# Hybrid decoder layer on one Trainium2 core: one 384-byte pair of buffers leaves an early pool, and a 0/1 matrix is loaded with the tables and rounded by GpSimd

## The chip, the cores and the metric

The kernel runs on one core of one Trainium2 chip. The metric is the device time of one execution in microseconds (us), as the median of several runs. Five engines work side by side, each on its own queue and in the order that the program gives it: TensorE (PE, matmul; its weight loads are a row of their own, PEld), VectorE (DVE), ScalarE (ACT), GpSimd (POOL) and SyncE (SP), which issues every DMA of this kernel.

## The reference

One layer (DEPTH is 1) over x of shape (1, 2048, 1024), float32. After an RMSNorm one projection gives 13 slices of 256 channels, which four token mixers share:

```
h = _rms_norm(x, pre_g)
proj = jnp.einsum('bsd,de->bse', h, w_in)
aq, ak, av, ag, bu, bv, bg, cx, cg, dq, dk, dv, dg = jnp.split(proj, N_IN_SLICES, axis=-1)
ya = _dilated_mixture(heads(aq), heads(ak), heads(av))
yb = _spatial_gating(bu, bv, sgu_g, sgu_w, sgu_b)
yc = _multiscale_pool(cx, pool_w, pool_scale)
yd = _retention(dq, dk, dv, ret_g)
y = jnp.concatenate([ya * jax.nn.silu(ag), yb * jax.nn.silu(bg),
                     yc * jax.nn.silu(cg), yd * jax.nn.silu(dg)], axis=-1)
return x + _rms_norm(jnp.einsum('bse,ed->bsd', y, w_out), post_g)
```

Mixer A, the one that matters here, is softmax attention with 4 heads of 64 channels, each in three dilations (1, 4, 16). The three results of a head are added with weights that come from their log-sum-exp values: `o = sum over g of softmax(lse)[g] * out[g]`.

## The kernel before

Everything is float32, and a product is made of three matmuls: each operand is split into a rounded high part (type float32r) and the low rest, and high*high, high*low and low*high are added in PSUM. A matrix whose entries are 0 and 1 needs no low part; it is only copied into a float32r tile.

Stage 1 (function bodies up to line 538) makes all projections, in two halves of 1024 tokens. `prologue` normalizes and transposes x into tiles `hh` and `hl` (pool `big`); `weights` (L237) loads a slice of w_in into `raw`, and ACT and DVE split it into `w128` or `w256`; `proj_t` (L257) multiplies with the weights as the stationary operand and 512 tokens of `hh` as the moving one, `proj_m` (L267) with `hh` stationary and 256 columns of weights moving. The last two parts of the second half are `c_mix` (L384: pooling on POOL, tiles `c_x` and `c_s`, then `c_pl` on DVE, L412) and `a_gate` (L328: SiLU of the gate into `ag_s`, stored to DRAM as `agd`, L334).

Stage 2 (L880 to L898) is the attention. `attention(p, tab)` does two heads: it loads `q2`, `k2a`, `k2b` and the values `att_v` of a head (L569 to L585, seven buffers of 8 KB under one tag), and calls `branch` for the dilations 4, 16 and 1. In a branch PE makes scores (`ps_s`), DVE adds the bias and takes the row maximum (L649), ACT takes the exponential (L651), PE transposes (`ps_pt`), ACT and DVE split the result into `pt_hi` and `pt_lo` (L658, L659), and PE multiplies with the values (`ps_o`). `att_p`, the tile of the probabilities, has six buffers under the tag `pr` of pool `p2`. After the third dilation `weigh` (L744) turns the statistics into weights: a row of small DVE operations on 128x16 and 128x48, among them the rounding of `ew` into `eh` (L761, L762), ending in tile `wt`.

`combine` (L768) spreads these weights over the channels: it transposes `wt` to `wr` (32 rows) and multiplies `wr` with `sel`, a 32 x 8 x 128 matrix of zeros and ones, `mm(F, sel[:, n % 8], wr[g], True, True)` (L784), and DVE multiplies the attention results with F. So `sel` is first needed when the first pair of heads is done. It is loaded between `attention(0, tab)` and `combine(0, ...)` (L887 to L890) in two halves: a DMA each into a 2 KB buffer of the tag `pr`, and a DVE copy each into `sel`. A pool gives the buffers of one tag out in the order of the program, so these two take their turn behind all `att_p` tiles of `attention(0, tab)`.

Between the attention's matmuls PE is given output projections that don't need mixer A: `partial(t)` (L841) for 9 of the 16 token tiles, each held back by `tc.issue_after` until a chosen matmul of `attention(1, tab)`. Its weights `wo` come from `out_weights` (L545): two DMAs of 512 KB into `wo_raw` (tag `z` of pool `p3`, two buffers of 4 KB), a rounding by ACT (L551) and a subtraction by POOL or DVE (L552). Stage 3 (from L900) combines the second pair and finishes all tiles in `final`.

The order on each queue is set by a list scheduler that plans with modelled durations: an instruction is written into its engine's queue when the plan has it ready, earlier lines of the program first. On the chip each engine then follows that order, and waits where an input is late. DMAs share eight completion semaphores in turn, so a DMA also waits until the eighth before it has landed.

Pools are stacked from both ends of a partition's memory. From the left stand `const`, `big`, `small`, and above them in stage 1 `pa`, `pd`, `p1`, in stage 2 `pm`, `p2`, in stage 3 `p4`; from the right `k1` in stage 1 and later `p3`, `po`, `pc`. A tile that takes over memory waits for the last use of the tiles that were there. As the program before is laid out (byte addresses in a partition): `small` 82560 to 85952, its last tag `eh` with two buffers of 192 bytes; `w256` at 118720; `raw` at 153536 and 157632; six 2 KB buffers of the tag `w2` (among them `c_y`, `ag_s`) from 169920; `w128` at 182208, 190400, 198592; `c_x` 206784 to 208896; `c_s` 208896 to 213120. On the right: `sel` 174304, `wt`, `wr`, `sga` up to 184288; `po` up to 208864; the two `z` buffers at 208864 and 212960; and of stage 1 `cm`, the table whose last reader is `c_pl`, at 214816.

Of the kernel before, what the change touches and what calls it, by code (L numbers as in the profile page):

```python
# [9 lines left out]
F32 = mybir.dt.float32  # L10
F32R = mybir.dt.float32r
# [7 lines left out]
P = 128  # L19
SEQ = 2048  # L20
DM = 1024
KT = DM // P
GRP = 512
# [10 lines left out]
C_ID, C_DEC, C_ZETA, C_XI, C_CD, C_INVP, C_CNT, C_SEL, C_MIX = 0, 128, 640, 896, 1152, 1408, 1410, 1442, 2466  # L34
# [6 lines left out]
B_PR, B_PT = 6, 3  # L41
# [47 lines left out]
def hymba(ctx: ExitStack, tc: tile.TileContext, x, pre_g, w_in, sgu_g, sgu_w, sgu_b, pool_w,  # L89
          pool_scale, ret_g, w_out, post_g, cmix, catt, out, dbg=None, npart=9, spread=(0.3, 0.95)):  # L90
    nc = tc.nc
    V, A, G, T, D = nc.vector, nc.scalar, nc.gpsimd, nc.tensor, nc.sync

    def r32(ap):
        return ap.bitcast(F32)
# [4 lines left out]
    def transpose(o, i, n=P):  # L100
        T.transpose(o, i, ident[:n, :n])  # L101
# [3 lines left out]
    small = ctx.enter_context(tc.tile_pool(name="small", bufs=2))  # L105
# [435 lines left out]
    p3 = ctx.enter_context(tc.tile_pool(name="p3", bufs=1, side="right", reuse_waits="tile"))  # L541
# [15 lines left out]
    def attention(p, tab):  # L557
        o01 = (big if p == 0 else po).tile([P, 2, SEQ], F32, tag="big" if p == 0 else "o01", name="att_o01")
        o2 = po.tile([P, SEQ], F32, tag="o2", name="att_o2")
        o = [o01[:, 0], o01[:, 1], o2]  # L560
        wt = pc.tile([P, 3, 2, 2, 2, 8], F32, tag="wt", bufs=1, name="wt")
        for s in range(2):
            h = 2 * p + s
            rows = slice(s * HD, (s + 1) * HD)
            other = slice((1 - s) * HD, (2 - s) * HD)
            q2 = pm.tile([P, SEQ], F32R, tag="m8", bufs=7, name="q2")
            k2a = pm.tile([P, SEQ], F32R, tag="m8", bufs=7, name="k2a")
            k2b = pm.tile([P, SEQ], F32R, tag="m8", bufs=7, name="k2b")
            D.dma_start(r32(q2[rows]), qk_d[0][p][rows, 0])  # L569
            D.dma_start(r32(q2[other]), qk_d[0][p][rows, 1])  # L570
            for z in (rows, other):
                D.dma_start(r32(k2a[z]), qk_d[1][p][rows, 0])
                D.dma_start(r32(k2b[z]), qk_d[1][p][rows, 1])
            for b, dil in enumerate(DILS):
                vt = pm.tile([P, 16, 2 * HD], F32R, tag="m8", bufs=7, name="att_v")
                dst = r32(vt)
                if dil == 1:
                    src = v_d[h].rearrange("(n t c) d -> c t n d", c=4, t=32)
                    for c in range(4):
                        D.dma_start(dst[c * 32:(c + 1) * 32], src[c])  # L580
                elif dil == 4:
                    D.dma_start(dst.rearrange("q (j c) d -> q j (c d)", j=4),
                                v_d[h].rearrange("(j q c) d -> q j (c d)", j=4, c=4))
                else:
                    D.dma_start(dst.rearrange("q r d -> q (r d)"), v_d[h].rearrange("(q r) d -> q (r d)", r=16))  # L585
                qb = q2
                if dil != 1:
                    qb = pm.tile([P, SEQ], F32R, tag="m8", bufs=7, name="q2b")
                    if dil == 4:
                        src = r32(q2).rearrange("p (j k c i) -> p c j k i", j=4, c=4, i=8)  # L590
                        dst = qb.rearrange("p (j c k i) -> p c j k i", j=4, c=4, i=8)
                        for c in range(4):
                            (V if c < 3 else G).tensor_copy(dst[:, c], src[:, c])
                    else:
                        V.tensor_copy(qb.rearrange("p (r w i) -> p r w i", r=16, i=8),
                                      r32(q2).rearrange("p (w r i) -> p r w i", r=16, i=8))
                if dil == 1:
                    sv = p2.tile([P, 3, 2, 16], F32, tag="sv", bufs=2, name="sv")
                    raw = p2.tile([64, P], F32, tag="sT", bufs=1, name="sraw")
                    D.dma_start(raw, st_d[h].rearrange("b z (n q) -> (b z n) q", q=P))  # L600
                    branch(h, dil, qb, k2a, k2b, vt, tab, o[b], sv[:, b])
                    weigh(sv, raw, wt[:, :, :, s])
                    continue
                st = p2.tile([P, 2, 16], F32, tag="stat", bufs=2, name="att_st")
                branch(h, dil, qb, k2a, k2b, vt, tab, o[b], st)
                keep_stats(h, b, dil, st)
        return o01, o2, wt
# [121 lines left out]
    def keep_stats(h, b, dil, st):  # L729

        pt = ps2.tile([P, GRP], F32, tag="t", bufs=N_T, name="ps_st")
        transpose(pt[:32, :P], st.rearrange("p z n -> p (z n)"))
        sT = p2.tile([32, P], F32, tag="sT", bufs=1, name="sT")
        V.tensor_copy(sT, pt[:32, :P])
        for z in range(2):
            dst, src = st_d[h][b, z], sT[z * 16:(z + 1) * 16]
            if dil == 4:
                for j in range(4):
                    D.dma_start(dst.rearrange("(j k c i) -> j c k i", j=4, k=16, c=4)[j],
                                src[j * 4:j * 4 + 4].rearrange("c (k i) -> c k i", i=8))  # L740
            else:
                D.dma_start(dst.rearrange("(w r i) -> r w i", r=16, i=8), src.rearrange("r (w i) -> r w i", i=8))

    def weigh(sv, raw, w):  # L744

        pt = ps2.tile([P, GRP], F32, tag="t", bufs=N_T, name="ps_sv")
        transpose(pt[:, :64], raw, 64)
        V.tensor_copy(sv[:, :2].rearrange("q b z n -> q (b z n)"), pt[:, :64])
        nm = small.tile([P, 16], F32, tag="nm", name="nm")
        V.tensor_tensor(nm, sv[:, 0, 0], sv[:, 1, 0], ALU.min)  # L750
        V.tensor_tensor(nm, nm, sv[:, 2, 0], ALU.min)
        df = small.tile([P, 3, 16], F32, tag="df", name="df")
        V.tensor_tensor(df, sv[:, :, 0], nm.unsqueeze(1).broadcast_to([P, 3, 16]), ALU.subtract)
        ew = small.tile([P, 3, 16], F32, tag="ew", name="ew")
        A.activation(ew, df, AF.Exp, scale=-1.0)
        V.tensor_tensor(df, ew, sv[:, :, 1], ALU.mult)
        V.tensor_tensor(nm, df[:, 0], df[:, 1], ALU.add)
        V.tensor_tensor(nm, nm, df[:, 2], ALU.add)
        V.reciprocal(nm, nm)
        V.tensor_tensor(ew, ew, nm.unsqueeze(1).broadcast_to([P, 3, 16]), ALU.mult)  # L760
        eh = small.tile([P, 3, 16], F32R, tag="eh", name="eh")  # L761
        V.tensor_copy(eh, ew)  # L762
        V.tensor_copy(w[:, :, :, 0], r32(eh).rearrange("q b (g n) -> q b g n", g=2))
        for b in range(3):
            V.tensor_tensor(w[:, b, :, 1], ew[:, b].rearrange("q (g n) -> q g n", g=2),
                            r32(eh[:, b]).rearrange("q (g n) -> q g n", g=2), ALU.subtract)
# [111 lines left out]
    pc = ctx.enter_context(tc.tile_pool(name="pc", bufs=1, side="right", reuse_waits="tile"))  # L878
    sel = pc.tile([32, 8, P], F32R, name="sel")
    with ExitStack() as c2:  # L880
        pm = c2.enter_context(tc.tile_pool(name="pm", bufs=1, reuse_waits="tile"))
        p2 = c2.enter_context(tc.tile_pool(name="p2", bufs=1, reuse_waits="tile"))
        ps2 = c2.enter_context(tc.tile_pool(name="ps2", bufs=2, space=PSUM, reuse_waits="tile"))
        tab = pm.tile([P, T_HEAD], F32, name="tab")
        D.dma_start(tab, catt)
        o = attention(0, tab)
        for z in range(2):  # L887
            raw = p2.tile([P, 4, P], F32, tag="pr", bufs=B_PR, name="sel_raw")[:32]
            D.dma_start(raw, cmix[:32, C_SEL + z * GRP:C_SEL + (z + 1) * GRP].rearrange("r (n m) -> r n m", m=P))
            V.tensor_copy(sel[:, z * 4:z * 4 + 4], raw)  # L890
        for i in (1, 2, 3):
            out_weights(i, V if i == 2 else G)
        combine(0, o, ps2, "t", False, range(0, SEQ, GRP), G)
        o = attention(1, tab)
        for t in range(npart):
            with tc.issue_after(marks[int(len(marks) * (t + spread[0]) / npart * spread[1])]):
                partial(t)
        out_weights(0, G)  # L898
# [13 lines left out]
    for i, t in enumerate(full):  # L912
        n = -(-len(have) // (len(full) - i))
# [30 lines left out]
```

## Time and profile before

| what | value |
|---|---|
| median of 3 runs | 1067.3 us |
| lowest and highest | 1065.59 and 1068.7 us |
| the profiled execution | 1072.46 us |
| its span, first to last instruction | 1070.8 us |
| mean granted TensorE clock | 0.977 |
| PE busy | 1013.1 us, 95% of the span |
| DVE, ACT, POOL busy | 521.2, 377.4, 226.5 us |
| DMA | 128.91 MB, mean 120 GB/s |

The page of the profile shows one execution. A busy row counts an instruction from its start to its modelled end, and matmuls overlap, so 95% does not mean that PE is at its peak. The chain is the work that ended last, followed back from the last instruction to what released each step. In timelines a row gives start, duration, engine, line, operation, output and inputs, count, and in brackets how long the engine stood idle before it and what it waited for. The granted clock is the share of TensorE's full clock that it was allowed. Stage 1 ends at about 690 us, stage 2 at about 940 us.

### The profile page before, as it was taken

To read this page: it belongs to the slowest core of one execution; us is meant where nothing else is said; L and a number is where in the kernel's file an instruction comes from. 1 tells how busy PE (TensorE), PEld (TensorE's weight loads), DVE (VectorE), ACT (ScalarE), POOL (GpSimd) and SP (SyncE) were. 2 spreads that over 40 slices of the span, in tenths; PEclk is the share of its full clock that TensorE was granted. 3 is DMA by queue.
4 is the path that set the end of the run, shared out by engine and by line. 5 is a ranking of instruction groups with operands and counts; after the bars stand their busy time and mean duration, and the time that the engine had idled before them with its cause. 6 is when DMAs were issued, how large, how long until landed. Compare 5 with 4: busy or idle time off the path is not lost.

```text
span 1070.8 us, 15827 instructions
## 1 busy us (share of the span) xinstructions
PE 1013.1 (95%) x5960; PEld 862.7 (81%) x5960; DVE 521.2 (49%) x1586; ACT 377.4 (35%) x871; POOL 226.5 (21%) x216
## 2 busy tenths in 40 slices
PE   5899999999999999999999999997989989999995
PEld 5888898888777988989898777786987979866774
DVE  7511215686323331031675312177766767737766
ACT  6320213132212331132211111397763878712231
POOL 2310002121133000002120134031115521213444
PEclk9999999999999999999999999997899989999998
DMA  8530222332323232041311650286475573445566
GB/s 279 145 98 21 79 80 79 119 119 63 115 78 89 89 99 59 1 144 44 109 60 39 155 175 28 72 215 174 100 213 129 140 226 76 140 153 178 172 246 216
DMA packets 111036, 128.91 MB, mean 120 GB/s; under 512 B 9904, under 2 KB 89008, under 8 KB 108912
## 3 DMA queue, kind: packets, MB, share of 16 engines
q1 hardware_dynamic: 110960, 127.90, 40.0%
q8 instruction: 47, 0.77, 0.3%
q14 instruction: 29, 0.24, 0.1%
HBM read 91.57 MB, written 36.31 MB: 119 GB/s over the span
## 4 chain that ended last, share of the span: by engine, by line
PE 82%; DMA 9%; DVE 5%; issue 1%; POOL 1%; ACT 1%; SPq 1%; DVEq 0%; POOLq 0%; ACTq 0%
PE ps_t L98 38%; PE ps_m L98 15%; PE ps_out L98 11%; PE ps_s L98 4%; PE ps_o L98 4%; PE ps_pt L101 3%; PE ps_of L98 2%; DMA k2b<-qk 2%; DMA out_dram<-z 1%; DMA cm<-in_cmix_dram 1%; DMA z<-partd 1%; DMA sel_raw<-in_cmix_dram 1%; DMA raw<-in_w_in_dram 1%; PE ps_in L98 1%; DVE z L872 1%
## 5 line engine op out<-in xcount | busy, mean ns | idle before, releaser
L98 PE MATMUL ps_t<-hh,w 128*128 128x512 f32 x1152 | 372.8, 400 | 0.0
L98 PEld LDWEIGHTS ps_t<-hh,w 128*128 128x128 f32 x1152 | 215.9, 188 | 54.0 <-issue 3.4
L98 PE MATMUL ps_t<-hl,w 128*128 128x512 f32 x576 | 229.0, 398 | 0.0
L98 PE MATMUL ps_m<-w,hh 128*128 128x256 f32 x1024 | 187.8, 283 | 3.8 <-ACT hh L232 3.8
L98 PEld LDWEIGHTS ps_m<-w,hh 128*128 128x128 f32 x1024 | 159.1, 190 | 5.4 <-ACT hh L232 4.4
L98 PE MATMUL ps_out<-wo,yt 128*128 128x512 f32 x576 | 156.6, 411 | 0.7 <-DVE z L872 0.6
L98 PE MATMUL ps_m<-w,hl 128*128 128x256 f32 x512 | 146.4, 286 | 0.1
L98 PEld LDWEIGHTS ps_t<-hl,w 128*128 128x128 f32 x576 | 108.3, 188 | 26.1 <-issue 1.4
L98 PEld LDWEIGHTS ps_out<-wo,yt 128*128 128x128 f32 x576 | 106.6, 194 | 24.8 <-issue 2.8
L252 DVE TENSOR_TENSOR w<-raw,w 128x1024 fp32r<-128x1024 f32 x42 | 58.4, 1399 | 110.6 <-ACT w L250 110.6
L98 PEld LDWEIGHTS ps_m<-w,hl 128*128 128x128 f32 x512 | 97.3, 190 | 0.7 <-DVE hl L233 0.3
L649 DVE CUSTOM_DVE_ANT_0 att_p<-ps_s,tab 128x128 f32<-128x128 f32 (+1 forms) x192 | 60.8, 360 | 39.1 <-PE ps_s L98 32.9
L250 ACT ACTIVATE w<-raw 128x1024 fp32r<-128x1024 f32 (+1 forms) x56 | 55.0, 997 | 70.3 <-PE ps_t L98 38.2
L659 DVE TENSOR_TENSOR pt_lo<-ps_pt,pt_hi 128x512 fp32r<-128x512 f32 x80 | 51.4, 651 | 18.2 <-ACT pt_hi L658 17.6
L651 ACT ACTIVATE att_p<-att_p,att_st 128x128 f32<-128x128 f32 (+1 forms) x128 | 55.0, 432 | 10.3 <-DVE att_st L649 9.9
L98 PE MATMUL ps_o<-pt_hi,att_v 128*128 128x128 f32 (+1 forms) x204 | 52.6, 280 | 3.1 <-DVE att_o L674 3.1
L98 PE MATMUL ps_o<-pt_lo,att_v 128*128 128x128 f32 (+1 forms) x204 | 52.3, 293 | 3.3 <-DVE pt_lo L659 3.3
L101 PE MATMUL ps_pt<-ident,att_p 128*128 128x128 f32 x300 | 50.9, 286 | 1.5 <-ACT att_p L651 1.3
L446 POOL TENSOR_TENSOR d_g<-d_g,ret_b 128x512 f32<-128x512 f32 x8 | 10.4, 1294 | 185.6 <-ACT d_g L444 185.6
L658 ACT ACTIVATE pt_hi<-ps_pt 128x512 fp32r<-128x512 f32 x80 | 44.2, 565 | 12.9 <-PE ps_pt L101 7.7
L98 PEld LDWEIGHTS ps_o<-pt_hi,att_v 128*128 128x128 f32 x204 | 40.2, 197 | 5.5 <-DVE att_o L674 3.6
L98 PEld LDWEIGHTS ps_o<-pt_lo,att_v 128*128 128x128 f32 x204 | 40.2, 197 | 5.0 <-DVE pt_lo L659 3.8
(174 smaller groups left out, 1414.3 us busy)
## 6 DMA issues: line engine op xcount, KB each, us to landing
raw<-in_w_in_dram SPq DMA_DIRECT2D x52, 512.0 KB
qk<-qk_s SPq DMA_DIRECT2D x16, 512.0 KB
att_v<-vd SPq DMA_DIRECT2D x8, 1024.0 KB
xr<-in_x_dram SPq DMA_DIRECT2D x16, 512.0 KB
out_dram<-z SPq DMA_DIRECT2D x15, 512.0 KB
xt<-in_x_dram SPq DMA_DIRECT2D x7, 1024.0 KB
yraw<-yb SPq DMA_DIRECT2D x16, 384.0 KB
partd<-z SPq DMA_DIRECT2D x9, 512.0 KB
```

Of the source, the lines that this page charges most:

```text
L98: return T.matmul(o, lhsT, rhs, start=start, stop=stop, skip_group_check=True)
L101: T.transpose(o, i, ident[:n, :n])
L250: A.activation(hi, raw[:, :, cs], AF.Copy, scale=sc)
L252: eng.tensor_tensor(lo, raw[:, :, cs], r32(hi), ALU.subtract)
L446: G.tensor_tensor(o, o, ret_b.unsqueeze(1).broadcast_to([P, 2, 256]), ALU.mult)
L649: V.tensor_tensor_reduce(out=pr[:, u, :w], in0=ps[:, u, :w], in1=bb, scale=-SLOPES[h] * HD ** -0.5, scalar=3e38, op0=ALU.add, op1=ALU.min, ...
L651: A.activation(pr[:, u, :w], pr[:, u, :w], AF.Exp, bias=neg, scale=-1.0, accum_out=st[:, 1, n:n + 1])
L658: A.activation(hi, pt[:, :w], AF.Copy)
L659: V.tensor_tensor(lo, pt[:, :w], r32(hi), ALU.subtract)
L872: V.scalar_tensor_tensor(z[:, ns], ps, rstd, post_b[:, ns], ALU.mult, ALU.mult)
```

## The change

`eh` leaves pool `small`, where it had two buffers, for pool `pc`, where it has one. Everything that is stacked above `small` on the left moves down by 384 bytes, the weights `w128` and `w256` of the projections among it, while `hh` and `hl` stay; on the right `pc` grows by 192 bytes. The load of `sel` goes from behind `attention(0, tab)` to a place ahead of it, next to the load of `tab`; it becomes one DMA of 32 rows of 4 KB into a buffer of the tag `z` of `p3`, and the two DVE copies become one POOL copy.

```
@@ weigh
-        eh = small.tile([P, 3, 16], F32R, tag="eh", name="eh")
+        eh = pc.tile([P, 3, 16], F32R, tag="eh", bufs=1, name="eh")
         V.tensor_copy(eh, ew)
@@ stage 2
         tab = pm.tile([P, T_HEAD], F32, name="tab")
         D.dma_start(tab, catt)
+        raw = p3.tile([P, DM], F32, tag="z", bufs=2, name="sel_raw")[:32]
+        D.dma_start(raw, cmix[:32, C_SEL:])
+        G.tensor_copy(sel, raw.rearrange("r (n m) -> r n m", m=P))
         o = attention(0, tab)
-        for z in range(2):
-            raw = p2.tile([P, 4, P], F32, tag="pr", bufs=B_PR, name="sel_raw")[:32]
-            D.dma_start(raw, cmix[:32, C_SEL + z * GRP:C_SEL + (z + 1) * GRP].rearrange("r (n m) -> r n m", m=P))
-            V.tensor_copy(sel[:, z * 4:z * 4 + 4], raw)
         for i in (1, 2, 3):
             out_weights(i, V if i == 2 else G)
```

## The prediction

> **What bounds the kernel now.** I read the page first, then the chain of waits in order of time, then the timelines of DVE, PE, SP and POOL where the chain leaves PE.
>
> ```profile
> span 1070.8 us, 15827 instructions
> PE 82%; DMA 9%; DVE 5%; issue 1%; POOL 1%; ACT 1%; SPq 1%; DVEq 0%; POOLq 0%; ACTq 0%
> ```
>
> PE carries 82% of the chain and DMA 9%. So a change pays in two ways only: PE does its work faster, or one of the few places goes where PE waits for something else. The chain in order of time names such a place, and it is the load that the change moves:
>
> ```profile
> 789.70 10.04 DMA sel_raw<-in_cmix_dram
> ...
> 799.76 0.75 DVE sel L890 x2
> ...
> 800.54 0.70 DVE pt_lo L659
> ...
> 801.28 1.22 PE ps_o L98 x4
> ```
>
> The reader sees a row of dependents: the load lands 10.04 us after its issue, only then can DVE round it into `sel`, only then does DVE reach the `pt_lo` that stood behind in its queue, and PE's `ps_o` waits for that. Nothing needs `sel` yet: its first matmul comes at 814.7, by the tile's own answer.
>
> ```profile
> L98 PE MATMUL ps_f<-wr,sel x32: 326/422/442, 814.7 to 992.0; 32*128 32x384 f32 x32
> ...
>   DMA sel_raw<-in_cmix_dram: 5.4, 1
> ```
>
> The same place in the timelines of DVE, ACT and PE gives the price to DVE and to PE (in brackets the idle time ahead and its end):
>
> ```profile
> 799.76 0.75 DVE L890 CAST sel<-sel_raw 32x512 fp32r<-32x512 f32 x2 [5.39 <-DMA sel_raw<-in_cmix_dram]
> 800.54 0.69 DVE L659 TENSOR_TENSOR pt_lo<-ps_pt,pt_hi 128x512 fp32r<-128x512 f32 x1
> ...
> 794.80 0.98 ACT L658 ACTIVATE pt_hi<-ps_pt 128x512 fp32r<-128x512 f32 x2 [1.15 <-PE ps_pt L101]
> ...
> 797.93 0.27 PE L98 MATMUL ps_o<-pt_hi,att_v 128*128 128x256 f32 x1
> 801.28 0.58 PE L98 MATMUL ps_o<-pt_lo,att_v 128*128 128x256 f32 x1 [3.08 <-DVE pt_lo L659]
> ```
>
> And the stretches around it, as columns PE, PEld, DVE, ACT, POOL busy, granted clock, DMA share, GB/s:
>
> ```profile
> 794.00:801.00 7.00, 4.21 (x29) 3.56 (x27) 1.58 (x4) 1.57 (x3) 0.00 (x0) 0.93 1.05 339
> 800.10:806.90 6.80, 5.62 (x21) 5.13 (x22) 6.64 (x27) 4.78 (x18) 0.00 (x0) 0.50 0.30 119
> 807.00:814.00 7.00, 7.00 (x40) 5.91 (x40) 4.23 (x19) 3.42 (x12) 3.04 (x4) 1.00 0.36 112
> ```
>
> PE is idle for 3.08 us, and for the next 6.8 us its granted clock is 0.50; from 807 on it is 1.00 again.
>
> The Trainium skill, TensorE: Matmul & The Clock Gate, section Part 1: The HAM clock gate, says that the clock is halved after at least one idle window of about 3.4 us. The idle here was 3.08 us and the halving came all the same, so an account by that length alone would leave the clock out and end at a gain of 3.1 us; the row shows 0.50, and I go by the row.
>
> **The change, part by part.**
>
> *The stall goes.* For DVE: `pt_lo` at 800.54 had its input when the first of two `pt_hi` ended, 794.80 + 0.98/2 = 795.3. It can start 800.54 - 795.3 = 5.2 us earlier (the wait of 5.39 and the two copies of 0.75, less some 0.9 in which DVE would have waited for ACT). For PE: the idle 3.08 us, and the half clock behind it, in which PE was busy for 5.62 us; the same matmuls at full clock take 2.81, so 2.8 more. That is 5.9 us on PE. The two meet again at the transposition of `wt`, which needs both DVE's row in `weigh` and PE's place in its queue, so the smaller counts: 5.2 us, up to 5.9 where PE alone decides, and 3.1 if the clock is halved anyway. I take 5.3.
>
> *What is late next there.* PE's own queue: from 801.28 the chain is PE's own work nearly throughout, until the next load of keys, and that is issued when PE releases the buffer, so it moves with PE:
>
> ```profile
> 829.07 1.05 PE ps_pt L101 x7
> ...
> 863.40 0.49 PE ps_o L98 x4
> 863.89 0.09 SPq L573
> ...
> 864.03 7.03 DMA k2b<-qk
> ```
>
> The values for the next head, issued just ahead of the old `sel` loads, land at about 799 at the latest (same queue, ahead of a load that landed at 789.70 + 10.04 = 799.74). The next head's first transposes are the row at 829.07, behind `combine`, and its values are wanted after them. They do not bind.
>
> *The load in its new place.* It needs the first `z` buffer, at 208864, which lies over both `c_s` buffers; their last reader is `c_pl`. POOL then writes `sel`, which lies over three `w2` buffers; of the stores from there the last is the second `agd`, issued after ACT's 679.59.
>
> ```profile
> 668.04 0.75 DVE L412 SCALAR_TENSOR_TENSOR c_pl<-c_s,cm,c_x 128x512 f32<-128x512 f32 x1 [2.60 <-POOL c_s L409]
> ...
> 679.59 1.17 ACT L333 ACTIVATE ag_s<-ps_t 128x512 f32<-128x512 f32 x1 [5.27 <-PE ps_t L98]
> ...
> 680.79 11.42 SPq L334 DMA_DIRECT2D agd<-ag_s  x3
> 692.30 0.89 SPq L550 DMA_DIRECT2D wo_raw<-in_w_out_dram  x2
> ...
> 694.20 0.93 SPq L813 DMA_DIRECT2D yraw<-yb  x2
> ...
> 667.40 0.60 POOL L409 COPY c_s<-c_s 64x512 f32<-64x512 f32 x1
> 700.76 0.95 POOL L825 CAST yt<-yraw 128x384 fp32r<-128x384 f32 x2 [32.75 <-DMA yraw<-yb]
> ...
> 790.11 0.61 POOL L593 CAST q2b<-q 128x512 fp32r<-128x512 f32 x1 [1.03 <-PE ps_s L98]
> ```
>
> So the load can run from 668.8, or at the latest where `wo_raw` stands now, 692.3, since both want a `z` buffer and it comes first in the program. POOL is idle from 668.0 to 700.76. Its copy has 1024 columns; the casts of 384 (0.95 for two) and 512 columns (0.61) differ by 0.13 for 128, which gives 0.61 + 4 x 0.13 = 1.1 us. It costs nothing while it ends before 700.76. If POOL were held, who waits is `yt` (partial projections) and, from 704, the low parts of `wo`.
>
> *The `z` buffers.* `sel_raw` takes the first, `wo_raw` the second, and the next `wo_raw` must wait for POOL's copy. ACT uses the pair back to back, the second at about 704.1:
>
> ```profile
> 703.08 1.99 ACT L551 ACTIVATE wo<-wo_raw 128x1024 fp32r<-128x1024 f32 x2
> ...
> 704.20 4.71 POOL L552 TENSOR_TENSOR wo<-wo_raw,wo 128x1024 fp32r<-128x1024 f32 x2 [0.54 <-ACT wo L551]
> ...
> 708.97 9.56 DMA wo_raw<-in_w_out_dram
> 718.54 0.54 DMA std<-sT
> ...
> 722.00 9.33 DMA k2b<-qk
> ```
>
> The load itself, issued at 692.3 as the latest, is bounded by `yraw`, issued at 694.20 and landed at 700.76, 6.6 us with some 2 MB in that queue; its 128 KB at the queue's front are a sixteenth of that, 0.4 us. I take 3 us: POOL ends near 696.5, the second `wo_raw` is issued some 4 us later than at 692.75 and has 7 us until 704.1, as long as `yraw` needed. So 0; by the upper bound POOL would end at 700.0 and the second `wo_raw` come 2.5 us late, which leaves 2.8 of the gain. Worse than that is a rival below.
>
> *The removed issues.* SP loses two DMA issues at 789.70 to 791.57 in a stretch where the DMA share is 1.05; the next load of values comes up to 1.9 us earlier. Not needed before 829.07, so 0. The new issue costs SP 0.4 us where SP waits for ACT.
>
> *`eh`.* Writer and readers are all DVE, in order, so one buffer adds no wait: 0. Its new bytes lie over a `w2` buffer of stage 1, free long before the first `weigh`.
>
> *The shift by 384 bytes.* The first matmuls of stage 1 and those of stage 2 read from quite different places, `w128` and `w256` above `small`, `yt` in `p3` on the right, and still:
>
> ```profile
> 57.81 39.20 PE ps_t L98 x168
> 97.01 22.61 PE ps_m L98 x192
> ...
> 830.12 1.63 PE ps_out L98 x7
> 850.11 1.40 PE ps_out L98 x6
> ```
>
> 39.20/168 = 233.3 ns for 512 columns with stationary `w128`; 1.63/7 = 232.9 and 1.40/6 = 233.3 with stationary `yt`; 22.61/192 = 117.8 for 256 columns with `w256` moving, half of it. No place is faster than another, so I take 0 for the shift.
>
> Sum: 1072.46 - 5.3 = 1067.2 for the profiled execution. That one lies 5.2 us above the median of the runs shown, 1067.3, so against the median the forecast is 1067.3 - 5.3 = 1062.0.
>
> **The rivals.** *No measurable change:* the stall goes and most of its time is lost again before the end. For: the plan of all queues from 690 on is made anew with other modelled times, and PE's later waits (k2b at 864.03 for 7.03 us) fall where they like; with the halved clock kept and one us lost, 1067.3 - 3.1 + 1 = 1065.2. Against: the chain from 801.28 to 863.9 is PE's own, and the load behind it is tied to PE's progress.
>
> *Slower, by a late pair of `z`:* were the new load planned last before 692.3 and to land as late as the old one (10.04 us), POOL would end at 692.3 + 10.04 + 1.1 = 703.4, the second `wo_raw` would be issued 10.7 us later than now, and with 9.56 us in flight land at 713; ACT's 1.0 and POOL's 2.4 behind it end at 716.5 instead of 708.91, 7.6 us later. The chain rows show what hangs on that: the next `wo_raw` at 708.97 gates the small stores of the statistics, these gate `k2a` and `k2b`, and PE waits for `k2b`. The result is 1067.3 - 5.3 + 7.6 = 1069.6. It decides from 5.3 us of delay on. Against it: at 692.3 only stores of stage 1 stand ahead, while the old load landed in a stretch whose DMA share was 1.05 at 339 GB/s.
>
> *The address matters after all:* projection matmuls are 53% of the span by the chain below, 38% `ps_t` (407 us at 233.3 ns, some 1740 of them) and 15% `ps_m` (161 us at 117.8, some 1360); one ns each is 3.1 us. 1.7 ns more each would use up the gain.
>
> ```profile
> PE ps_t L98 38%; PE ps_m L98 15%; PE ps_out L98 11%; PE ps_s L98 4%; PE ps_o L98 4%; PE ps_pt L101 3%; PE ps_of L98 2%; DMA k2b<-qk 2%; DMA out_dram<-z 1%; DMA cm<-in_cmix_dram 1%; DMA z<-partd 1%; DMA sel_raw<-in_cmix_dram 1%; DMA raw<-in_w_in_dram 1%; PE ps_in L98 1%; DVE z L872 1%
> ```
>
> If the rate now is held back by where the weights lie, the bound is the half-clock rows:
>
> ```profile
> 801.66 0.41 PE L98 MATMUL ps_o<-pt_hi,att_v 128*128 128x256 f32 x1
> ...
> 802.09 0.41 PE L98 MATMUL ps_o<-pt_hi,att_v 128*128 128x256 f32 x1
> ```
>
> Two matmuls of 256 columns in 0.43 us at clock 0.50 are 107.5 ns each at full clock, against 117.8: 9% of 568 us, up to 50 us faster, 1017. The same page of the Trainium skill, in the same section, gives 215.7 ns between matmuls of 512 columns at full clock; here it is 233.3, and no row shows why. The equal pace from three pools speaks against an address as the cause.
>
> *The change doesn't do what it says:* DVE stood for another reason and only the name is that of `sel`. Then 1067.3. The landing at 799.74 and the start at 799.76 leave little room.
>
> **How the numbers follow.** 0.3% or 3.2 us is about what a measurement of this kernel tells from no change. Full gain (1060.5 to 1064): 0.56. Gain mostly lost or stall only renamed (1064.1 to 1067.5, a little above): 0.18. Slower by the late `z` or a worse plan behind 690 (1068 to 1072): 0.13. Address: faster 0.04, slower 0.02. A plan behind 690 that is better beyond the stall (1057 to 1060): 0.07. Faster: 0.56 + 0.04 + 0.07 = 0.67; same 0.18; slower 0.15. The range for 8 in 10 reaches from the better plan into the late-`z` case: 1057.5 to 1068.5; the likeliest case alone has 1060.5 to 1064.
>
> **What would show it.** Right: the rows of `sel` stand before 700, as one POOL cast of about 1.1 us ahead of `yt`; no DVE wait for `sel_raw`; at the place that is now 794 to 807 no PE idle of 3 us and a granted clock of 1.00; the load of keys that is now at 864.03 some 5 us earlier; `ps_t` still 233 ns apart. Wrong: POOL's `yt` or `wo` later than 701 and 709, a wait of SP for the copy, the `k2b` that now lands at 731.3 (722.00 + 9.33) later, or another spacing of `ps_t` and `ps_m`.

## The result, and the profile after

The changed kernel takes 1057.5 us (median of 7 runs) against 1067.7 us of the kernel before (7 runs); the ratio is 0.9919, with a 95% interval from 0.9899 to 0.9939. One run of the changed kernel took 1063.4 us, at a granted clock of 0.934, and the others 1055.4 to 1060.0; further down, one execution of 3416.8 us (the shift alone) and one of 1404.1 us (the load alone) are left out of the medians. The forecast was 1062.0, with a range from 1057.5 to 1068.5: the direction is right, the gain of 10.2 us is about twice the 5.3 that were forecast, and the time stands at the very edge of the range.

The page of the changed kernel, first lines and the row of the granted clock:

```profile
span 1055.3 us, 15826 instructions
...
PE 1003.0 (95%) x5960; PEld 860.1 (82%) x5960; DVE 519.7 (49%) x1584; ACT 377.0 (36%) x871; POOL 228.3 (22%) x217
...
PEclk9999999999999999999999999997999989998998
```

The moved load is where the prediction put it. The timeline of SP and POOL in the changed kernel, behind stage 1:

```profile
681.55 0.32 SPq L334 DMA_DIRECT2D agd<-ag_s  x1
681.96 0.38 SPq L887 DMA_DIRECT2D sel_raw<-in_cmix_dram  x1
682.41 0.41 SPq L550 DMA_DIRECT2D wo_raw<-in_w_out_dram  x1
...
683.81 0.90 SPq L813 DMA_DIRECT2D yraw<-yb  x2
685.42 1.03 POOL L888 CAST sel<-sel_raw 32x1024 fp32r<-32x1024 f32 x1 [27.22 <-ACT att_p L651]
686.48 0.33 SPq L550 DMA_DIRECT2D wo_raw<-in_w_out_dram  x1
690.30 0.95 POOL L825 CAST yt<-yraw 128x384 fp32r<-128x384 f32 x2 [3.84 <-DMA yraw<-yb]
```

POOL's copy takes 1.03 us and is over at 686.45; `yt` behind it waits for its own load, not for POOL. But all this stands 10 us earlier than it did, and that is the finding: stage 1, which has nothing to do with the load, is shorter. The last instructions of stage 1 and the two loads that PE waits for next, in the changed kernel's chain:

```profile
605.20 22.26 PE ps_t L98 x96
...
665.73 14.68 PE ps_t L98 x64
680.42 1.11 ACT ag_s L333
...
698.64 9.87 DMA wo_raw<-in_w_out_dram
...
712.03 9.05 DMA k2b<-qk
```

The same pieces in the chain of the kernel before:

```profile
675.77 14.95 PE ps_t L98 x64
690.75 1.13 ACT ag_s L333
...
708.97 9.56 DMA wo_raw<-in_w_out_dram
...
722.00 9.33 DMA k2b<-qk
```

Stage 1's last step, `ag_s`, starts at 680.42 instead of 690.75, 10.3 us earlier; `wo_raw` and `k2b` are 10.3 and 10.0 us earlier, so the gain is carried through the first loads of stage 2. The last 64 `ps_t` show where it is made: 14.68/64 = 229.4 ns each, and 14.95/64 = 233.6 before. The matmuls themselves follow each other faster.

Columns of the next two rows: stretch, length, busy time (and instructions) of PE, PEld, DVE, ACT, POOL, granted clock, DMA share, GB/s. The first is of the kernel before, the second of the changed one:

```profile
55.00:680.00 625.00, 624.42 (x3729) 531.62 (x3728) 227.28 (x588) 134.75 (x190) 96.44 (x103) 1.00 0.28 84
```

```profile
55.00:680.00 625.00, 623.90 (x3772) 535.92 (x3771) 226.98 (x588) 136.40 (x190) 97.34 (x103) 1.00 0.28 85
```

PE is busy for the whole stretch in both and the clock is 1.00 in both, but the changed kernel gets 43 more matmuls into it. A faster pace of an engine that is never idle does not show in its busy share; it shows in the count beside it.

### The profile page after: what moved, and what is told of

It reads as the page before. It is cut to its first block, busy times and chain, and to the rows that moved or that the text cites. A ratio compares the mean times of both kernels' runs of the same rounds, so it can differ in the third digit from the quotient of the medians.

```text
span 1055.3 us, 15826 instructions
## 1 busy us (share of the span) xinstructions
PE 1003.0 (95%) x5960; PEld 860.1 (82%) x5960; DVE 519.7 (49%) x1584; ACT 377.0 (36%) x871; POOL 228.3 (22%) x217
## 5 line engine op out<-in xcount | busy, mean ns | idle before, releaser
L98 PE MATMUL ps_t<-hh,w 128*128 128x512 f32 x1152 | 369.0, 397 | 0.4 <-DVE b_t L372 0.4
L98 PE MATMUL ps_t<-hl,w 128*128 128x512 f32 x576 | 227.1, 394 | 0.0
L98 PE MATMUL ps_m<-w,hh 128*128 128x256 f32 x1024 | 183.6, 282 | 4.0 <-ACT hh L232 4.0
L446 POOL TENSOR_TENSOR d_g<-d_g,ret_b 128x512 f32<-128x512 f32 x8 | 10.3, 1288 | 181.4 <-ACT d_g L444 181.4
L874 POOL TENSOR_TENSOR z<-z,xr 128x1024 f32<-128x1024 f32 x15 | 35.9, 2393 | 32.3 <-DVE z L872 21.8
```

The lines of the kernel that those rows point to most:

```text
L98: return T.matmul(o, lhsT, rhs, start=start, stop=stop, skip_group_check=True)
L446: G.tensor_tensor(o, o, ret_b.unsqueeze(1).broadcast_to([P, 2, 256]), ALU.mult)
L874: (V if last else G).tensor_tensor(z[:, ns], z[:, ns], xr[:, ns], ALU.add)
```

## The experiments

In all of them "distance" is the address of the stationary operand's tile minus that of the moving one, within a partition, modulo 512, by the program's allocation. For `ps_t` that is `w128 - hh` (`hl` has the same remainder as `hh` except where told): 320 before, 448 after. For `ps_m` it is `hh - w256`: 192 before, 64 after. For `ps_out` it is `yt - wo`, and so on. Mean spacings are worked out from the start times of neighbouring matmuls of one kind (some 1626 pairs of `ps_t` and 1423 of `ps_m` in each profile); before they are 233.31 and 117.77 ns, after 229.15 and 114.71.

**The shift alone.** The kernel before, and only the small tile moved:

```
-        eh = small.tile([P, 3, 16], F32R, tag="eh", name="eh")
+        eh = pc.tile([P, 3, 16], F32R, tag="eh", bufs=1, name="eh")
```

> The kernel before with the one edit at eh: the weights stand 384 bytes lower, sel is still loaded behind the first pair of heads. Theory S+A (two gains that add up: the moved load of sel is worth about 5 us, the new place of the weights the rest): ps_t matmuls of 512 columns start 229.2 ns apart instead of 233.3, ps_m 114.7 instead of 117.8, the last ag_s begins near 680 us instead of 690.75; the DVE wait for sel_raw stays, 4 to 6 us; in all 5 to 10 us faster than before. Rival R (the closer spacing belongs to the run or the chip, not to the place): 233.3 and 117.8 again, no change beyond 0.3%.

Median 1055.95 us against 1065.32 of the kernel before on that chip, ratio 0.9927 [0.9911, 0.9944]. `ps_t` follow each other at 229.14 ns, `ps_m` at 114.52, the last `ps_t` starts at 680.3. The old load of `sel` is still there, and DVE still waits for it, for 3.0 us:

```profile
L889 SPq DMA_DIRECT2D sel_raw<-in_cmix_dram x2: 419/494/568, 775.0 to 775.6; - x2
L890 DVE CAST sel<-sel_raw x2: 407/411/415, 782.6 to 783.0; 32x512 fp32r<-32x512 f32 x2
...
  DVE sel L890: 3.0, 1
```

PE loses 0.64 us to the `pt_lo` behind it. So the shift alone gives the whole gain, as far as the intervals tell (0.9927 here, 0.9919 for the whole change), and with the wait of DVE left in.

**The load alone.** The changed kernel with `eh` back in its old pool, the opposite edit.

> The changed kernel with eh back in the early pool: all tiles on the left stand as before, sel is loaded early. Theory S+A: spacing 233.3 and 117.8 as before, the DVE wait for sel_raw and the 3 us idle of PE behind it are gone, 4 to 6 us faster than before. Rival R: it is as fast as the changed kernel, about 10 us faster, since only the load matters and the spacing comes and goes. Rival P (the plan of the queues is what moved): anything between, with other waits of PE than in the changed kernel.

Median 1064.46 us, ratio 0.9995 [0.998, 1.001]. `ps_t` at 233.31 ns, `ps_m` at 117.66, last `ps_t` at 689.0. The load is moved, DVE and PE no longer wait for it, and the median shows no gain; the interval leaves room for 2 us at most.

**The kernel before, profiled once more.** Why is a stall of 5 us worth nothing?

> The kernel before, unchanged, profiled a second time. Theory T (the first profile caught an untypical execution, 1072.46 us against a median of 1067.7: the load of sel was late in it): DVE waits 1 to 4 us for sel_raw, PE has no idle of more than 1.5 us there and no half clock, and the execution is 3 to 6 us shorter than the one profiled first. Theory M (the stall is in every execution, and e2 lost its gain elsewhere): again over 5 us of DVE wait, 3 us of PE idle and half a clock behind it.

This execution took 1067.78 us, 4.7 less than the one that the prediction was made from. The timelines of SP, DVE and PE at the same place:

```profile
785.61 1.12 SPq L889 DMA_DIRECT2D sel_raw<-in_cmix_dram  x2
...
790.76 0.30 PE L98 MATMUL ps_s<-k2a,q2b 128*128 128x128 f32 x1
...
793.21 0.78 DVE L890 CAST sel<-sel_raw 32x512 fp32r<-32x512 f32 x2 [2.92 <-DMA sel_raw<-in_cmix_dram]
...
794.02 0.69 DVE L659 TENSOR_TENSOR pt_lo<-ps_pt,pt_hi 128x512 fp32r<-128x512 f32 x1
...
794.76 0.39 PE L98 MATMUL ps_o<-pt_lo,att_v 128*128 128x256 f32 x1 [0.64 <-DVE pt_lo L659]
...
803.68 0.38 PE L101 MATMUL ps_w<-ident,wt 128*32 128x128 f32 x2 [1.20 <-DVE wt L765]
```

And the stretches around it:

```profile
785.00:793.00 8.00, 8.00 (x55) 7.19 (x54) 4.55 (x12) 4.43 (x11) 0.61 (x1) 1.00 1.03 310
793.00:800.00 7.00, 6.10 (x35) 4.98 (x34) 6.67 (x25) 4.41 (x16) 0.49 (x1) 1.00 0.41 165
800.00:807.00 7.00, 5.80 (x35) 4.86 (x34) 4.77 (x21) 3.91 (x14) 2.53 (x4) 1.00 0.38 131
```

The load lands 7.6 us after its issue, not 10.0; DVE waits 2.92 us, not 5.39; PE loses 0.64 us, not 3.08; and the granted clock stays at 1.00. The idle 3.08 us and the half clock are in neither of the two other executions with the old load: in that of the shift alone the load lands 7.6 us after its issue as well, and PE loses 0.64 us too.

What the moved load is worth at this place can be read from the traces, since the matmuls of PE come in the same order in all kernels of this document. The stretch from one matmul ahead of the stall, the first `ps_s` in these rows, to the first `ps_w` behind it, in the first profile of the kernel before and, below, with the load alone:

```profile
794.84 0.30 PE L98 MATMUL ps_s<-k2a,q2b 128*128 128x128 f32 x1
...
810.82 0.38 PE L101 MATMUL ps_w<-ident,wt 128*32 128x128 f32 x2
```

```profile
790.61 0.30 PE L98 MATMUL ps_s<-k2a,q2b 128*128 128x128 f32 x1
...
802.09 0.38 PE L101 MATMUL ps_w<-ident,wt 128*32 128x128 f32 x2 [1.21 <-DVE wt L765]
```

It is 15.98 us in the first profile, 12.92 in the second and 12.93 with the shift alone; with the load alone it is 11.48, and 11.4 to 11.5 in all other kernels with the moved load. So the moved load does gain something there: 4.5 us in an execution like the first, 1.45 in one like the other two. That 1.45 us reaches the end of the kernel is not shown.

Nor was the stall what made the first profile long. At that `ps_s`, ahead of the stall, it was already 4.1 us behind the second (794.84 and 790.76), at `ps_w` 7.1, and at the end 4.7. Of the 4.1 us, 0.5 arose in stage 1; the rest is not explained.

In the changed kernel PE's wait at this place is that for `wt`, 1.20 us, which is also in this profile of the kernel before:

```profile
792.36 0.34 DVE L765 TENSOR_TENSOR wt<-ew,eh 128x16 f32<-128x16 f32 x3
...
792.68 0.38 PE L101 MATMUL ps_w<-ident,wt 128*32 128x128 f32 x2 [1.20 <-DVE wt L765]
```

**Everything moved by 384 bytes.** What in the shift counts: where `w128` and `w256` lie, or where they lie as seen from `hh`? The changed kernel with 384 more bytes in the lowest pool, so that the weights have the remainders of the kernel before again and `hh` moves along.

```
-    ident = cp.tile([P, P], F32, name="ident")
+    ident = cp.tile([P, P + 96], F32, name="ident")[:, :P]
```

> The changed kernel with 384 bytes added in the first pool on the left, so hh, wo and the weights all move up: the weights stand at 182208 as in the kernel before, but as far from hh as in the changed kernel. Theory A-rel (what counts is how the two operands of a matmul stand to each other): ps_t 229.2 ns and ps_m 114.7. Theory A-abs (what counts is the address of the weights alone, modulo 512): 233.3 and 117.8 as before. Neither: another value.

1051.64 us in one run; `ps_t` 229.16 ns, `ps_m` 114.83, as in the changed kernel. The distance counts, not the address.

**64 bytes more.** The changed kernel with 64 more bytes in `small`: distance 0 for `ps_t` and for `ps_m`.

```
-            rstd = small.tile([P, 16], F32, tag="lnr", name="lnr")[:, :8]
+            rstd = small.tile([P, 24], F32, tag="lnr", name="lnr")[:, :8]
```

> The changed kernel with 64 bytes added at the end of pool small: hh stays, the weights move up by 64, to the same remainder modulo 512 as hh (128). Theory A-rel: ps_t and ps_m change again by 1 ns or more, in a direction that I don't know; a smooth dependence would put them below 229.2 and 114.7, since the kernel before stood 192 bytes from such a match and the changed one stands 64 from it. Rival (only the old place is bad, all others are alike): 229.2 and 114.7.

1060.83 us in one run. Rows of its chain, and below them those of the changed kernel (from its second profile, further down):

```profile
57.11 38.11 PE ps_t L98 x168
95.22 23.03 PE ps_m L98 x192
...
141.74 23.23 PE ps_m L98 x192
```

```profile
57.54 38.47 PE ps_t L98 x168
96.01 21.78 PE ps_m L98 x192
...
141.44 21.97 PE ps_m L98 x192
```

The kernel before has 39.20 and 22.61 in the same pieces, as the prediction quotes them. For `ps_t` the three are 233.3, 229.0 and 226.8 ns, for `ps_m` 117.8, 113.4 and 119.9. The same 64 bytes make one kind of matmul faster and the other slower.

**Three scans of the distance.** The first makes all tiles of `big` 64 bytes longer (and `small` by 64 in all), so that `hh` and `hl` have different remainders, and each buffer of `w128` 128.

> The changed kernel with all buffers kept and their distances altered: the four big slots (hh, hl, wo) are 64 bytes more than a multiple of 512 apart, the three w128 slots 128 more, and pool small is 64 bytes longer. So ps_t meets eight remainders of (weights minus hh) modulo 512, ps_m four. Theory A-rel: the spacing of a matmul is a function of that remainder alone, whichever slots make it up: at 0 227.6 ns, at 448 229.2, at 320 233.3 (ps_t), and for ps_m, hh minus w256, at 0 119.8; new values for the rest, up to 6 ns apart, some perhaps below 227. Rival A-slot (it is a matter of single addresses, not of the remainder): the same remainder made up by other slots gives other values, by more than 1 ns.

1063.79 us; sorted by the distance of their own two operands, all `ps_t` lie between 230.7 and 232.1 ns, without the order expected. With `hh` and `hl` at two remainders the distance of the single matmul does not foretell its spacing. The next two keep `hh` and `hl` alike and give the three buffers of `w128` three distances in one run. The edit of the first is below; beside it `small` grows by 128 bytes in the first and by 256 in the second, 64 and 128 for each of its two buffers, and these are the numbers that the two expectations name:

```
-                w = p1.tile([P, 2, KT, n], F32R, tag="w128", bufs=3, name="w128")
+                w = p1.tile([P, 2 * KT * n + 16], F32R, tag="w128", bufs=3, name="w128")[:, :2 * KT * n].rearrange("p (l k n) -> p l k n", l=2, k=KT)
```

> The changed kernel, with 64 more bytes in small and each of the three w128 buffers 64 bytes longer, so that the remainder of (w128 - hh) by 512 is 64, 128 and 192 in turn, while hh and hl keep the same remainder as each other. Known for one remainder at all three buffers: 320 gives 233.3 ns between ps_t, 448 gives 229.2, 0 gives 227.6. Theory A (the spacing depends smoothly on that remainder): the matmuls of the three buffers have three different spacings, the one at 64 near 227 to 230 and those at 128 and 192 higher, towards 232 to 234. Theory B (there are only two or three good places, of which 448 and 0 are two): all three at 233 +- 0.5. Theory C (the pair that matters is not the stationary operand and the moving one, but something with a whole group): no difference between the three buffers, one value for all. ps_m has hh - w256 = 448 here; known: 192 gives 117.8, 64 gives 114.7, 0 gives 119.8; I expect 115 to 118. Time between 1050 and 1068.

> The changed kernel, with 128 more bytes in small, 64 in p1, and each of the three w128 buffers 128 bytes longer, so that the remainder of (w128 - hh) by 512 is 256, 384 and 0 in turn. Theory A (a smooth dependence on that remainder): 0 comes out near 227.6 ns, 256 and 384 near 231 to 234. Theory B (few good places): 0 at 227.6, the others at 233 +- 0.5. Theory C: one value for all three buffers. ps_m has hh - w256 = 320 here; I expect 116 to 119. Time between 1052 and 1068.

Groups of 24 `ps_t` share a buffer. The timeline of PE in the first of the two; each row is the second matmul of a group:

```profile
63.42 0.39 PE L98 MATMUL ps_t<-hl,w 128*128 128x512 f32 x1
...
74.41 0.39 PE L98 MATMUL ps_t<-hl,w 128*128 128x512 f32 x1
...
85.57 0.40 PE L98 MATMUL ps_t<-hl,w 128*128 128x512 f32 x1
...
91.17 0.39 PE L98 MATMUL ps_t<-hl,w 128*128 128x512 f32 x1
```

Two groups at distance 192 take 74.41 - 63.42 = 10.99 us, 229.0 ns a matmul; two at 128 take 11.16 us, 232.5 ns; one at 64 takes 5.60 us, 233.3 ns. In the second scan:

```profile
62.79 0.39 PE L98 MATMUL ps_t<-hl,w 128*128 128x512 f32 x1
...
73.69 0.40 PE L98 MATMUL ps_t<-hl,w 128*128 128x512 f32 x1
...
84.83 0.39 PE L98 MATMUL ps_t<-hl,w 128*128 128x512 f32 x1
...
90.27 0.39 PE L98 MATMUL ps_t<-hl,w 128*128 128x512 f32 x1
```

Distance 0: 227.1 ns, 384: 232.1, 256: 226.7. The times were 1065.43 and 1061.04 us, one run each. Means over all `ps_t` of each distance, over the whole profile:

| distance of `w128` from `hh`, bytes modulo 512 | 0 | 64 | 128 | 192 | 256 | 320 | 384 | 448 |
|---|---|---|---|---|---|---|---|---|
| ns between `ps_t` | 227.6 | 233.3 | 232.4 | 229.4 | 227.9 | 233.3 | 232.4 | 229.2 |

The two halves of the row agree within 0.3 ns: the pattern repeats every 256 bytes. It is not smooth (64 is among the worst), and it is not a matter of 0 and 448 alone (192 and 256 are good too), so neither theory on record holds as it was put. `ps_out` of the last stage, whose operands are other tiles, agrees without having been aimed at: 227.4 ns at 0 (the run with 64 more bytes), 233.3 at 64 and 229.2 at 192 (the two scans), 233.3 at 320 and 229.2 at 448 (the kernel before and the changed one). Steps finer than 64 bytes were not scanned, and the row can't be read between its columns: `ps_out` of the partial projections stands 233.1 ns apart at 480, with everything moved by 384 bytes, though 448 and 0 on either side are good. `ps_m` came out at 117.8 ns at 448 and at 117.2 at 320, within what was expected. The kernel before stood at one of the two worst distances, the changed one stands on a middle step.

**Using it.** Three kernels on one chip: the changed kernel again, the same with 64 bytes ahead of `w128` alone (distance 0 for `ps_t`, and `w256` where it was), and that one with two more small tiles that bring `yt` to distance 256 in the partial projections and to 0 in the last stage. The first pair of lines is the edit of the second kernel; the third has all of them.

```
-                        sq = p1.tile([P, DM], BF16, tag="sq", bufs=1, name="sq")
+                        sq = p1.tile([P, DM + 32], BF16, tag="sq", bufs=1, name="sq")[:, :DM]
...
+    p4.tile([P, 16], F32, name="pad4")
...
+    p3.tile([P, 24], F32, name="pad3")
```

> The changed kernel unchanged, as the yardstick for the two kernels beside it: 1057 +- 2, ps_t 229.2 ns, ps_m 114.7, ps_out of the partial projections 233.6, of the last stage 229 to 230.

> The changed kernel with 64 more bytes ahead of w128 alone, so that (w128 - hh) has remainder 0 while hh - w256 keeps 64. Theory (the spacing of matmuls hangs on the remainder of the distance between the two operands): ps_t 227.6 instead of 229.2, ps_m unchanged at 114.7; 1728 matmuls x 1.6 ns = 2.7 us less than the changed kernel. Rival (ps_m's 119.8 in the run with 64 more bytes throughout came from w128's place, or from the sum of all): ps_m goes to 119.8 again and the time is 5 us over this.

> As the kernel before it, and with 64 bytes ahead of the last stage's tiles (yt, ya, ysa - wo: remainder 0) and 96 bytes behind yt in p3 (yt - wo: remainder 256, from 352). The theory foretells a third kind of matmul that no change has touched so far: ps_out of the partial projections 227.9 ns instead of 233.6 (some 300 matmuls, 1.7 us), ps_out of the last stage 227.5 instead of 229 to 230 (some 460, 0.8 us), ps_t 227.6, ps_m 114.7. Sum: some 5 us under the changed kernel. Rival (remainders of w128 alone matter, or yt in p3 is held by something else): partial projections stay at 233.6.

| kernel | median us | ratio to the kernel before | `ps_t` ns | `ps_m` ns | `ps_out` ns, partial / last stage |
|---|---|---|---|---|---|
| changed, again | 1054.81 | 0.9898 [0.9875, 0.992] | 229.1 | 114.6 | 233.6 / 229.1 to 229.4 |
| `w128` up 64 | 1054.23 | 0.9875 [0.9851, 0.9898] | 227.5 | 115.6 | 233.7 / 229.1 to 229.3 |
| three places | 1055.66 | 0.9892 [0.9872, 0.9912] | 227.6 | 115.6 | 229.7 / 227.1 to 227.5 |

`ps_t` and `ps_out` of the last stage came out as foretold. `ps_out` of the partial projections, at 233.1 to 233.8 in the kernels till then (the first scan aside), moved the right way but less far (229.7 for 227.9 foretold), and `ps_m` did not stay at 114.7. The times did not follow: the three intervals overlap, so no kernel here is shown to beat the changed one. One reason is in the chain of the second kernel:

```profile
57.77 38.11 PE ps_t L98 x168
95.88 22.61 PE ps_m L98 x192
...
141.95 21.97 PE ps_m L98 x192
```

`ps_t` is at its best, but the first piece of `ps_m` is back at 22.61 (117.8 ns) although neither `w256` nor `hh` has moved; the second is at 21.97. At one and the same distance `ps_m` runs at either of two paces. Stage 1 ends at 677.8 by its last `ps_t`, against 679.1 in the changed kernel beside it: 2.8 us (1728 matmuls by 1.6 ns) less 1.5 (1536 by 1.0 ns).

The other reason is that what lies behind stage 1 varies more than these gains. From the last `ps_t` to the end of the span it took 380.4 and 376.3 us in the two profiles of the kernel before, 371.2 with the load alone, 369.5 with the shift alone, 375.3 and 373.7 in the changed kernel, 369.4 with everything moved by 384 bytes, 374.0 and 376.1 in the last two. In this spread the 1.45 us of the moved load can't be seen either: the shortest but one has the old load in it.

## Why the prediction was right, and where it was wrong

**The sum: right in sign, from the wrong term.** All of the forecast gain, 5.3 us, was the stall at `sel`; the load alone measured 0.9995 [0.998, 1.001], and 1.45 us in its own stretch. The gain measured is that of the shift, which stood in the sum as 0 and measured 0.9927 alone. That the time still lies at the edge of the range is luck: the range reached down to there for a better plan of the queues behind 690 us, and PE's order is the same before and after.

**The step "the stall goes".** The rows were read rightly for the execution they came from; the step that failed is the next, to take a stall out of one profiled execution and subtract it from the median of others. For that execution the price was not far off: its stretch is 4.5 us longer than with the moved load, for the 5.3 worked out. In the two other executions with the old load it is 1.45 us longer, so the term was over three times too large for the median. The prediction noted that this execution was 5.2 us above the median and did not ask whether its stall was in the others. The 5.2 us and the stall are not the same time, close as the two numbers are: most of the lag was there ahead of the stall. Of the rivals, "no measurable change" is what the load alone did; the loss behind it that this rival supposed is not shown.

**The step "the shift by 384 bytes: I take 0".** It argued that three pools at quite different addresses show the same 233 ns. They do, but the address is not what counts. By the allocation the distances were 320 (`w128`) and 352 (`yt` in `p3`), both on the upper step of the pattern, and `ps_out` of the last stage stood at 320 too. Equal results from places that agree in the hidden variable say nothing about it. The rival "the address matters after all" was the right one, at a chance of 0.04 for faster; its own price, 3.1 us for each ns, gives with 4.16 ns for `ps_t` and 3.06 for `ps_m` 1728 x 4.16 + 1536 x 3.06 = 7.2 + 4.7 = 11.9 us, against 10.3 by which stage 1 ended earlier. The estimate is on the high side, since not every one of these matmuls follows its neighbour at this pace.

What the runs showed for `ps_t` leaves the bound of that rival, 215 ns for 512 columns, unreached: the best distance gives 226.7 in undisturbed groups. The half-clock rows from which it was taken are matmuls of another kind, so they need not be a measure for these.

**The load in its new place, the `z` buffers, `eh`.** Right. The load was issued at 681.96 and POOL's copy ran from 685.42, so it was in flight for at most 3.5 us, where 3 was taken; the copy took 1.03 us for the 1.1 worked out; the second `wo_raw` was issued 4.07 us after the first (682.41 and 686.48) for "some 4"; and no idle time of DVE stands ahead of the rows of `eh`. The late pair of `z`, the rival on the slow side, did not come.

**What was to show it.** The row of `sel` and the missing wait came as told. "`ps_t` still 233 ns apart" came out wrong, and the text had named another spacing as the sign of its error; that sign led to the cause. Another sign of error came too, and meant nothing: SP waited 1.2 us for POOL's copy ahead of the second `wo_raw`, a delay that the sum itself had put at no cost. The load of keys told of at 864.03 stands at 853.98 with the load alone, but at 856.90 in the second profile of the kernel before, so its move of "some 5 us" can't be laid to the change.

## What to carry to other kernels

Before pricing a stall seen in one profile, profile the same kernel again and measure the same stretch, from one named matmul to another, in both: only what the stall costs in most executions can be gained. Where an execution lies above the median, don't take its most visible stall for the reason. Where PE is busy throughout, count matmuls in a stretch rather than read the busy share, and after any change to a pool compare the spacing of matmuls that the change did not mean to touch. A few bytes of padding that move the stationary against the moving operand are a cheap thing to try, one kind of matmul at a time.

## What the runs showed of the hardware

Not expected: the pace of back-to-back float32r matmuls at full granted clock (1.00 from 55 to 680 us) depends on the distance between their two operands in memory. At the eight distances tried it goes from 227.6 to 233.3 ns for 512 columns, and it repeats after 256 bytes. Over some 1728 matmuls that is 10 us between the best and the worst. The Trainium skill, SBUF — State Buffer, section Who interferes with whom, says that PE and ACT never wait on anyone; these runs do not contradict it if it is read as of other engines, but PE's own pace is not free of where its two operands lie. Whether the stationary operand that counts is a matmul's own or that of the next one can't be told, as both have the same remainder here, and which part of the memory or of PE makes the steps was not tried.

`ps_m` stays partly open. Its groups run at one of three paces, about 113.3, 117.7 and 120.0 ns. At distance 0 all were near the last and at 192 nearly all at the middle one; at 64 groups of the same kernel stand at the first and at the middle one, and moving `w128` alone changed which. Even one kernel differs from execution to execution: five neighbouring groups of the kernel before, from 365 us on, stand at about 118 ns in the first profile and at 113.3 in the second, with the same addresses. So a second cause beside the distance sets it, perhaps in how a group starts; no run told it apart. Nor does the distance explain `ps_t` where `hh` and `hl` have different remainders.

And a granted clock of 0.50 for 6.8 us followed an idle time of 3.08 us in one execution of the kernel before, while the next profile of the same kernel has neither; what lies behind stage 1 spread over 369 to 380 us from one profile to the next.
